# A decoder block with seven-product matmuls: sums of weight quarters made in DRAM for 54 units, and the first FFN block put in another order

## The chip, the core and the metric

The kernel runs on one core of a Trainium2 chip. The metric is the time of one execution on the device, in microseconds (us); lower is better. The core has five engines with an instruction queue each: TensorE (PE: matmuls; PEld: its weight loads), VectorE (DVE), ScalarE (ACT), GpSimd (POOL) and SyncE (SP). Data moves between DRAM and on-chip memory by DMA; here SP issues nearly all loads, POOL the stores of intermediate results and every DMA that adds to what its target holds.

## The reference

A decoder block for 512 rows of width 2048, in fp32. An input projection (2048 to 4096) feeds two token mixers (a gMLP spatial gate and an RG-LRU recurrence); their outputs go through an output projection. The channel mixer, which takes most of the time, is a GeGLU MLP with a causal convolution of width 3:

```python
h = _rmsnorm(x, norm2_g[l])
up = jnp.einsum('bsd,df->bsf', h, ffn_w_up[l])          # 2048 -> 12288
up = _causal_dwconv(up, ffn_conv_w[l], ffn_conv_b[l])
gate, val = jnp.split(up, 2, axis=-1)
x = x + jnp.einsum('bsf,fd->bsd', jax.nn.gelu(gate) * val, ffn_w_down[l])   # 6144 -> 2048
return _rmsnorm(x, final_g)
```

## The kernel before

**The mixers** (lines 240 to 563). Eight projections of 2048 x 512 and four output projections run as matmuls of 512 columns. In the first one (line 278) the rows of `xT`, the weights `w_in`, their splits and the squares for the norm all arrive piece by piece, and TensorE works on each as it comes (`load_rows`, lines 257 to 274; the loads alternate on SP's queue, lines 140 and 263).

**Precision.** Every fp32 operand is split into a rounded high part (`h`, a cast on ACT, line 115) and the rest (`l`, a subtraction on DVE, line 116), and each product is three matmuls.

**Seven products instead of eight.** In the FFN both operands are cut into 2 x 2 quarters, and a scheme of the Strassen-Winograd kind forms seven products of sums of quarters. A *unit* is one tile pair: 7 products x 2 halves x 3 matmuls of 256 columns (line 800), 42 matmuls. There are 280 units: 192 for the up projection (24 blocks of 8, gate and value in turn) and 88 for the down projection, in three chunks of 8, 8 and 6 row tiles by four column blocks. The last part of the down projection (lines 948 to 998) is plain matmuls.

**Operands.** A weight unit (class `Weights`) has a buffer `q` of eight slots: the four quarters of the weight in slots 4 to 7 and four sums in slots 0 to 3. `load` (line 579) issues the loads on SP, `sums` (line 587) makes the sums on DVE: lines 590 (two at once, 512 columns), 591 and 592 (256 each). `pair` (line 594) splits slots 0 to 6 into high and low parts of 1792 columns. Activations (class `Acts`) go the same way with differences (lines 615 to 617); for the first block they are filled by transposes on TensorE of the normed rows and a copy by ACT (`from_rows`, lines 706 and 708), for the down chunks loaded from `ad`, the DRAM buffer of gated activations. There are three buffers of `q` and three of the split weights, taken in turn.

**Sums made in DRAM.** For the last 96 units (184 to 279) the two sums of line 590 are not made on DVE: POOL copies two quarters into a DRAM tile `made` and adds the fourth quarter to both by an accumulating DMA (line 686), 256 KB each. One such DMA is issued per up unit, from unit 0 on, each adding one waiting for its copy. `load` then brings 256 KB from `made` and 384 KB from the weights.

**Order.** One list, `stream`, holds all operands in the order in which they are prepared. `prepare` (line 655) walks it: for each, load one ahead, sums one ahead, pair it, load two ahead. In the FFN each engine's queue is in the order in which this is written (line 773). The activations of a new chunk are spread over the units around the change, by `spread` (line 721); this and the units 0 to 7 are the three *changes of operand* and the *first up block*. Before the first block, units 0 to 2 are prepared during the output projection (line 760). Outside the part with a written order a scheduler places instructions; that holds for POOL at the start, too, where it puts the first `made` pieces ahead of the gate weights `graw` (line 336) of the recurrence.

Of the kernel before, what the change touches and what calls it, by code (L numbers as in the profile page):

```python
# [8 lines left out]
F32 = mybir.dt.float32  # L9
# [3 lines left out]
ALU = mybir.AluOpType  # L13

P = 128
S = 512
# [27 lines left out]
NG = 12  # L44
NP = 24

CHUNKS = [range(0, 8), range(8, 16), range(16, 22)]
TAIL = 22
# [15 lines left out]
EVAC = 150  # L64


@with_exitstack
def hybrid_block(ctx: ExitStack, tc: tile.TileContext, x, xT, w_in, w_out, w_up, w_dn, w_us, w_ds, w_dl, wab, wsT, vec, bs, vgb, fg, out):
# [399 lines left out]
    for i in range(2):  # L468
        for st in range(NS):
            t = vv[i][:, st]  # L470
# [97 lines left out]
    pools = {"t": pool("ts", "right")}  # L568

    def slots(name, n=8):  # L570
        return wq.tile([P, n, 256], F32, name=name, tag=name)

    class Weights:
# [5 lines left out]
        def load(self):  # L579
            self.q = q = slots("q")  # L580
            if self.made is None:
                nc.sync.dma_start(q[:, 4:8], self.src)
            else:
                nc.sync.dma_start(q[:, 2:4], self.made)
                nc.sync.dma_start(q[:, 4:7], self.src[:, 0:3])

        def sums(self):
            q = self.q
            if self.made is None:
                nc.vector.tensor_tensor(q[:, 2:4], q[:, 5:7], q[:, 7:8].broadcast_to([P, 2, 256]), ALU.add)  # L590
            nc.vector.tensor_tensor(q[:, 1], q[:, 2], q[:, 6], ALU.add)  # L591
            nc.vector.tensor_tensor(q[:, 0], q[:, 1], q[:, 4], ALU.add)  # L592

# [6 lines left out]
    class Acts:  # L600
# [45 lines left out]
    stream = []  # L646
    halves = []
    place, a_place = {}, {}
    done = [0, 0, 0]
# [18 lines left out]
    units = [(w_up[g + NG * v, m], m) for g, v in ups for m in range(8)]  # L668
    starts = []
    made = {}  # L670
# [3 lines left out]
    n_up = starts[0]  # L674


    sums_src = [w_us[m] for m in range(8)] + [w_ds[n, p] for c in CHUNKS for n in range(4) for p in c]
    for k, src in enumerate(sums_src):
        made[n_up - 8 + k] = tc.dram_tile([32, 2048], F32, name=f"made{k}")

    def make(u):

        k = u // 2
        if k < len(sums_src):
            how = {"accum_op": ALU.add, "max_dma_last_dim": 8192} if u % 2 else {"max_dma_last_dim": 8192}
            nc.gpsimd.dma_start(made[n_up - 8 + k], sums_src[k][u % 2], **how)  # L686

    def act_tiles(m, shape):
        a = pools["a2" if m == 7 else "a1"]
# [2 lines left out]
    def scale_rows(d):  # L692
        for st in range(NS):
            t = x2[d][:, st]
            if d < 2:
                nc.vector.tensor_scalar(t, t, rstd2[:, st:st + 1], None, ALU.mult)
            else:
                nc.scalar.mul(t, t, rstd2[:, st:st + 1])
# [38 lines left out]
    last_w = [Plain([w_dl[d].rearrange("p (a b) -> p a b", a=8)], half_tiles(i)) for i, d in enumerate(DORD)]  # L737
    for u, (src, _) in enumerate(units):
        place[u] = len(stream)
        stream.append(Weights(src, made[u].rearrange("(p b) (c d e) -> (p b c) d e", p=32, c=4, d=2) if u in made else None))  # L740
# [87 lines left out]
    def up_block(g, val, u0):  # L828
        q = {}
        for m in range(8):  # L830
            prepare(ready(u0 + m))
            for p in ORDER:
                product(q, p, act[m], stream[place[u0 + m]].hl, True, m == 0, m == 7)
                if p == 6:
                    rest_of_loads()
            make(u0 + m)
            if m == 7 and u0 == 0:
                pads[:] = [t_tile(f"pad{n}", [P, 2, S + 2]) for n in range(2)]
                for t in pads:
# [37 lines left out]
        for i, (n, j) in enumerate(((1, 0), (1, 1), (0, 0), (0, 1))):  # L877
            f = 48 * val + 4 * g + 2 * n + j
# [78 lines left out]
    for st in range(NS):  # L957
# [22 lines left out]
        v, y, u, r = (const.tile([P, 1], F32, name=f"r3{c}", tag=f"r3{c}", bufs=2) for c in "vyur")  # L980
# [80 lines left out]
```

## Time and profile before

| | us |
|---|---|
| median of 3 runs | 2106.33 (2104.26 to 2107.17) |
| the profiled execution | 2107.67, its span 2106.0 |
| TensorE matmul busy | 2048.9 (97%) |
| DVE busy | 1746.8 (83%) |
| ACT busy | 911.5 (43%) |
| mean granted TensorE clock | 0.987 |
| DMA, both directions | 338.08 MB, 161 GB/s on average |

Stages in the trace: mixers to about 562 us, first up block from 576 to 641, up blocks to about 1540, down blocks to 2051, the plain end to 2106. Busy time of TensorE comes from modelled ends of pipelined matmuls (284 ns each where they follow one another every 120 ns), so it says little; the number of matmuls in a window of known length says how far TensorE was held up. The granted clock tells when it ran at half speed. A row of the chain of waits has a start, a length and the engine, tile and line that the end of the program depended on then.

### The profile page before, as it was taken

To read this page: it belongs to the slowest core of one execution; us is meant where nothing else is said; L and a number is where in the kernel's file an instruction comes from. 1 tells how busy PE (TensorE), PEld (TensorE's weight loads), DVE (VectorE), ACT (ScalarE), POOL (GpSimd) and SP (SyncE) were. 2 spreads that over 40 slices of the span, in tenths; PEclk is the share of its full clock that TensorE was granted. 3 is DMA by queue.
4 is the path that set the end of the run, shared out by engine and by line. 5 is a ranking of instruction groups with operands and counts; after the bars stand their busy time and mean duration, and the time that the engine had idled before them with its cause. 6 is when DMAs were issued, how large, how long until landed. Compare 5 with 4: busy or idle time off the path is not lost.

```text
span 2106.0 us, 34882 instructions
## 1 busy us (share of the span) xinstructions
PE 2048.9 (97%) x14488; PEld 1928.0 (92%) x14488; DVE 1746.8 (83%) x2249; ACT 911.5 (43%) x899; POOL 185.9 (9%) x310
## 2 busy tenths in 40 slices
PE   9999999999889999999999999999988998999998
PEld 7888888888679999999999999999988998999996
DVE  7588972735379999999999999999989788778876
ACT  6445322413264444444444444444454344444443
POOL 1000000000010111111111112112110000000001
PEclk9999999999899999999999999999998999999999
DMA  8222322434133656556557557557565555645663
GB/s 276 89 84 95 102 100 100 160 104 166 70 103 118 175 152 185 163 161 188 155 166 195 161 156 200 152 156 198 164 190 175 206 177 193 233 163 202 231 235 120
DMA packets 91647, 338.08 MB, mean 161 GB/s; under 512 B 12768, under 2 KB 13408, under 8 KB 75616
## 3 DMA queue, kind: packets, MB, share of 16 engines
q1 hardware_dynamic: 71712, 236.60, 33.9%
q0 software_dynamic: 19200, 98.58, 17.0%
q8 instruction: 113, 1.85, 0.4%
q10 hardware_dynamic: 576, 0.66, 0.1%
q14 instruction: 46, 0.38, 0.1%
HBM read 304.34 MB, written 81.79 MB: 183 GB/s over the span
## 4 chain that ended last, share of the span: by engine, by line
PE 84%; DVE 10%; DMA 4%; issue 1%; ACT 1%; SPq 0%; DVEq 0%; ACTq 0%
PE qs L800 56%; PE ps L153 9%; PE ps L152 9%; PE ps L151 9%; DVE wl L116 3%; DVE al L116 2%; DMA q<-ad 1%; DMA q<-w_dn 1%; DMA q<-w_up 1%; DVE q L591 1%; DVE q L615 1%; PE qs L152 1%; PE qs L153 1%; PE qs L151 1%; DVE q L592 0%
## 5 line engine op out<-in xcount | busy, mean ns | idle before, releaser
L800 PE MATMUL qs<-al,wh 128*128 128x256 f32 x2688 | 763.8, 284 | 3.6 <-DVE al L116 3.5
L800 PE MATMUL qs<-ah,wh 128*128 128x256 f32 x2688 | 764.4, 284 | 2.7 <-DVE pad L817 1.8
L800 PE MATMUL qs<-ah,wl 128*128 128x256 f32 x2688 | 763.4, 284 | 2.8 <-DVE wl L116 2.8
L115 ACT CAST wh<-q 128x1792 fp32r<-128x1792 f32 (+1 forms) x282 | 476.7, 1691 | 651.1 <-PE qs L800 474.6
L116 DVE TENSOR_TENSOR wl<-q,wh 128x1792 fp32r<-128x1792 f32 (+1 forms) x282 | 567.9, 2014 | 55.4 <-ACT wh L115 55.1
L800 PEld LDWEIGHTS qs<-al,wh 128*128 128x128 f32 x2688 | 518.8, 193 | 4.5 <-DVE al L116 4.5
L800 PEld LDWEIGHTS qs<-ah,wh 128*128 128x128 f32 x2688 | 518.8, 193 | 3.2 <-DVE pad L817 2.0
L800 PEld LDWEIGHTS qs<-ah,wl 128*128 128x128 f32 x2688 | 518.7, 193 | 3.2 <-DVE wl L116 3.2
L800 PE MATMUL qs<-wh,ah 128*128 128x256 f32 x1232 | 353.7, 287 | 11.0 <-ACT cc L913 4.5
L800 PE MATMUL qs<-wl,ah 128*128 128x256 f32 x1232 | 353.7, 287 | 7.4 <-DVE wl L116 7.4
L800 PE MATMUL qs<-wh,al 128*128 128x256 f32 x1232 | 352.9, 286 | 3.9 <-DVE al L116 3.9
L800 PEld LDWEIGHTS qs<-wh,ah 128*128 128x128 f32 x1232 | 240.9, 196 | 12.2 <-ACT cc L913 4.9
L800 PEld LDWEIGHTS qs<-wl,ah 128*128 128x128 f32 x1232 | 240.9, 196 | 9.2 <-DVE wl L116 9.2
L800 PEld LDWEIGHTS qs<-wh,al 128*128 128x128 f32 x1232 | 240.8, 195 | 4.3 <-DVE al L116 4.3
L116 DVE TENSOR_TENSOR wl<-wraw,wh 128x1024 fp32r<-128x1024 f32 (+2 forms) x105 | 118.2, 1126 | 147.6 <-ACT wh L115 147.2
L115 ACT CAST wh<-wraw 128x1024 fp32r<-128x1024 f32 (+2 forms) x105 | 102.2, 975 | 272.2 <-PE ps L152 141.0
L151 PE MATMUL ps<-xgh,wh 128*128 128x512 f32 x384 | 152.5, 398 | 0.1
L152 PE MATMUL ps<-xgl,wh 128*128 128x512 f32 x384 | 152.2, 397 | 0.0
L153 PE MATMUL ps<-xgh,wl 128*128 128x512 f32 x384 | 150.5, 397 | 0.1
L591 DVE TENSOR_TENSOR q<-q 128x256 f32<-128x256 f32 x280 | 118.6, 424 | 29.7 <-DMA q<-w_dn 20.1
L686 POOL DMA_DIRECT2D made<-w_ds x176 | 115.3, 755 | 283.0 <-DMA made<-w_ds 273.8
L590 DVE TENSOR_TENSOR q<-q 128x512 f32<-128x512 f32 x184 | 126.1, 685 | 6.4 <-DMA q<-w_up 6.2
(244 smaller groups left out, 2418.5 us busy)
## 6 DMA issues: line engine op xcount, KB each, us to landing
q<-w_up SPq DMA_DIRECT2D x184, 512.0 KB, 3.6
made<-w_ds POOLq DMA_DIRECT2D x176, 256.0 KB, 4.4
q<-w_dn SPq DMA_DIRECT2D x88, 384.0 KB, 3.3
wraw<-w_in SPq DMA_DIRECT2D x28, 1024.0 KB, 4.8
q<-made SPq DMA_DIRECT2D x96, 256.0 KB, 2.6
wraw<-w_out SPq DMA_DIRECT2D x16, 1024.0 KB, 4.8
ad<-gate POOLq DMA_DIRECT2D x48, 256.0 KB, 2.4
q<-ad SPq DMA_DIRECT2D x24, 512.0 KB, 3.3
```

Of the source, the lines that this page charges most:

```text
L115: nc.scalar.copy(h, src)
L116: nc.vector.tensor_tensor(l, src, h.bitcast(F32), ALU.subtract)
L151: nc.tensor.matmul(ps, lhsT=ah, rhs=bh, start=start, stop=False)
L152: nc.tensor.matmul(ps, lhsT=ah, rhs=bl, start=False, stop=False)
L153: nc.tensor.matmul(ps, lhsT=al, rhs=bh, start=False, stop=stop)
L590: nc.vector.tensor_tensor(q[:, 2:4], q[:, 5:7], q[:, 7:8].broadcast_to([P, 2, 256]), ALU.add)
L591: nc.vector.tensor_tensor(q[:, 1], q[:, 2], q[:, 6], ALU.add)
L615: nc.vector.tensor_tensor(q[:, 2:4], q[:, 7:8].broadcast_to([P, 2, 256]), q[:, 5:7], ALU.subtract)
L686: nc.gpsimd.dma_start(made[n_up - 8 + k], sums_src[k][u % 2], **how)
L800: nc.tensor.matmul(q[p][:, t], lhsT=x_, rhs=y_, start=first and t == 0 and n == 0, stop=last and t == 1 and n == 2, skip_group_check=True)
```

## The change

1. For 54 units all four sums are made in DRAM: units 0 to 7, and around each chunk's start the eight units before it and the chunk's first column block. Their tile `made` has 512 KB, put together by four DMAs on POOL: a copy of 512 KB and additions of 512, 256 and 128 KB. Their `load` brings 512 KB from `made` and 384 KB of quarters, and `sums` does nothing. The other 50 units of the last 88 keep two sums, as before. Pieces of four units take turns, so that an addition does not directly follow the piece on which it waits.
2. The 32 pieces for units 0 to 7 are issued at the kernel's start; the other 284 two per up unit.
3. In the first block a second operand of activations is built and a third begun before the first product; the scalings of two further row groups come one operand later; 40 matmuls into an unused bank (`idle`) stand ahead of the first transposes.
4. `spread` is denser: the eight activations of a new chunk take 11 units instead of 13.

```diff
+def made_units():
+    n_up = 24 * 8
+    starts = [n_up + 4 * (c[0] - CHUNKS[0][0]) for c in CHUNKS]
+    whole = list(range(8))
+    for c, s in zip(CHUNKS, starts):
+        whole += range(s - 8, s + len(c))
+    end = starts[-1] + 4 * len(CHUNKS[-1])
+    return whole, [u for u in range(n_up, end) if u not in whole]
...
-                nc.sync.dma_start(q[:, 2:4], self.made)
+                nc.sync.dma_start(q[:, 4 - self.made.shape[1]:4], self.made)
                 nc.sync.dma_start(q[:, 4:7], self.src[:, 0:3])
...
                 nc.vector.tensor_tensor(q[:, 2:4], q[:, 5:7], q[:, 7:8].broadcast_to([P, 2, 256]), ALU.add)
+            elif self.made.shape[1] == 4:
+                return
             nc.vector.tensor_tensor(q[:, 1], q[:, 2], q[:, 6], ALU.add)
...
-            if self.fill is not None and self.m in (1, 3):
-                scale_rows(2 + self.m // 2)
+            if self.fill is not None and self.m in (2, 4):
+                scale_rows(1 + self.m // 2)
...
-    def make(u):
-
-        k = u // 2
-        if k < len(sums_src):
-            how = {"accum_op": ALU.add, "max_dma_last_dim": 8192} if u % 2 else {"max_dma_last_dim": 8192}
-            nc.gpsimd.dma_start(made[n_up - 8 + k], sums_src[k][u % 2], **how)
+    for k, u in enumerate(whole):
+        t = tc.dram_tile([P, 4, 256], F32, name=f"made{u}")
+        made[u], rows[u] = t, [
+            (t.rearrange("(a b) c d -> a (b c d)", b=2), w_m4[k, 0:512].rearrange("(a b) c -> a (b c)", b=8)),
+            (t.rearrange("(a b) c d -> a (b c d)", b=2), w_m4[k, 512:1024].rearrange("(a b) c -> a (b c)", b=8)),
+            (t[:, 0:2], w_m4[k, 1024:1280].rearrange("(p a) c -> p a c", p=P)),
+            (t[:, 0], w_m4[k, 1280:1408]),
+        ]
...
+    for i in range(8, len(order), 4):
+        group = order[i:i + 4]
+        to_make += [(r, *rows[u][r]) for r in range(4) for u in group if r < len(rows[u])]
+    start_make = [(r, *rows[u][r]) for r in range(4) for u in order[:8]]
+
+    def make(todo, n):
+
+        for _ in range(min(n, len(todo))):
+            r, dst, src = todo.pop(0)
+            how = {"accum_op": ALU.add} if r else {}
+            nc.gpsimd.dma_start(dst, src, max_dma_last_dim=8192, **how)
+
+    make(start_make, len(start_make))
...
-    spread = (0, 2, 3, 5, 7, 9, 10, 12)
+    spread = (0, 1, 3, 4, 6, 7, 9, 10)
...
+    idle = pools["tr"].tile([P, S], F32, name="tr", tag="tr")
+    for _ in range(40):
+        nc.tensor.matmul(idle[:, 0:256], lhsT=stream[0].hl[0][:, 0, 0:P], rhs=stream[0].hl[0][:, 1], start=True, stop=True)
     first = a_place[0]
     stream[first].load()
...
     rest_of_loads()
-    done[:] = [first + 2, first + 1, first + 1]
+    stream[first + 1].sums()
+    stream[first + 1].pair()
+    stream[first + 2].load()
+    done[:] = [first + 3, first + 2, first + 2]
...
-            make(u0 + m)
+            make(to_make, 2)
```

The host hands over copies of the weight quarters in the order in which the pieces read them (`w_m4`, `w_m2`); it adds nothing up.

How the change moves instructions is shown at three places. Lines in rows of the changed kernel are its own; a number behind a name tells buffers apart.

POOL's queue at the start, before (`made` is the DRAM tile of sums, `graw` the gate weights of the recurrence, `pad` the zeroed edge of a convolution buffer):

```order
L686 DMA made_3491<-w_us 32x2048
masks.py:199 ISA
masks.py:199 AFFINE_SELECT ident<-ident 128x128
L686 DMA made_3491<-w_us 32x2048
L686 DMA made_3492<-w_us 32x2048 x2
L686 DMA made_3493<-w_us 32x2048 x2
L686 DMA made_3494<-w_us 32x2048 x2
L336 DMA graw<-wab 128x256
L313 MEMSET pad 128x3 x4
L336 DMA graw<-wab 128x256 x4
```

And in the changed kernel:

```order
L717 DMA made0_3491<-w_m4 64x2048
masks.py:199 ISA
masks.py:199 AFFINE_SELECT ident_88<-ident_88 128x128
L717 DMA made1_3492<-w_m4 64x2048
...
L717 DMA made7_3498<-w_m4 64x2048
L717 DMA made0_3491<-w_m4 64x2048
...
L717 DMA made5_3496<-w_m4 64x2048
L347 DMA graw_590<-wab 128x256
...
L347 DMA graw_702<-wab 128x256
L717 DMA made6_3497<-w_m4 64x2048
```

Eight pieces of 256 KB stood ahead of the first gate weights; now eight copies and six additions of 512 KB do. Behind the second `graw` stand the remaining 18 pieces of units 0 to 7 and four copies for units 184 to 187, and only then the third `graw`.

DVE in the first block, before (`al`, `wl`: low parts of activations and weights; sums of weights are lines 590 to 592, of activations 615 to 617):

```order
L116 TENSOR_TENSOR al2_4302<-q_4269,ah2_4301 128x1792
L615 TENSOR_TENSOR q_4305<-q_4305 128x512
L616 TENSOR_TENSOR q_4305<-q_4305 128x256
L617 TENSOR_TENSOR q_4305<-q_4305 128x256
L116 TENSOR_TENSOR wl_4365<-q_4296,wh_4364 128x1792
L590 TENSOR_TENSOR q_4368<-q_4368 128x512
L591 TENSOR_TENSOR q_4368<-q_4368 128x256
L592 TENSOR_TENSOR q_4368<-q_4368 128x256
L116 TENSOR_TENSOR al3_4374<-q_4305,ah3_4373 128x1792
```

And in the changed kernel:

```order
L127 TENSOR_TENSOR al2_4372<-q_4301,ah2_4371 128x1792
L628 TENSOR_TENSOR q_4379<-q_4379 128x512
L629 TENSOR_TENSOR q_4379<-q_4379 128x256
L630 TENSOR_TENSOR q_4379<-q_4379 128x256
L127 TENSOR_TENSOR wl_4440<-q_4365,wh_4439 128x1792
L127 TENSOR_TENSOR al3_4447<-q_4379,ah3_4446 128x1792
```

The three sums of the weight unit are gone from between the split of a weight and the split of an activation.

TensorE at the start of the first block, before (`tr` is the bank of the transposes, `qs` that of a product):

```order
L706 MATMUL tr_4183<-ident_88,x2_2805 128x128 x4
L706 MATMUL tr_4189<-ident_88,x2_2805 128x128 x4
L706 MATMUL tr_4207<-ident_88,x2_2805 128x128 x4
L706 MATMUL tr_4213<-ident_88,x2_2805 128x128 x4
L800 MATMUL qs_4219<-ah0_4202,wh_3987 128x256
```

And in the changed kernel:

```order
L812 MATMUL tr_4216<-wh_4023 128x256 x40
L739 MATMUL tr_4258<-ident_88,x2_2805 128x128 x4
L739 MATMUL tr_4264<-ident_88,x2_2805 128x128 x4
L739 MATMUL tr_4282<-ident_88,x2_2805 128x128 x4
L739 MATMUL tr_4288<-ident_88,x2_2805 128x128 x4
L739 MATMUL tr_4302<-ident_88,x2_3053 128x128 x4
L840 MATMUL qs_4308<-ah0_4277,wh_4023 128x256
```

The 40 idle matmuls come first, and the first transposes of the third operand now stand ahead of the first product; before, three transposes stood between unit 0 and unit 1, and now one does.

More of the change, by code (lines that the diff above doesn't have):

```diff
@@ L64, with hybrid_block @@
 EVAC = 150
+def made_units():
[6 more added lines that the diff above has]
+    return whole, [u for u in range(n_up, end) if u not in whole]
 @with_exitstack
-def hybrid_block(ctx: ExitStack, tc: tile.TileContext, x, xT, w_in, w_out, w_up, w_dn, w_us, w_ds, w_dl, wab, wsT, vec, bs, vgb, fg, out):
+def hybrid_block(ctx: ExitStack, tc: tile.TileContext, x, xT, w_in, w_out, w_up, w_dn, w_m4, w_m2, w_dl, wab, wsT, vec, bs, vgb, fg, out):
     nc = tc.nc
@@ L739, in hybrid_block @@
         place[u] = len(stream)
-        stream.append(Weights(src, made[u].rearrange("(p b) (c d e) -> (p b c) d e", p=32, c=4, d=2) if u in made else None))
+        stream.append(Weights(src, made.get(u)))
         for a in after.get(u, ()):
@@ L1021, in quarters, with made @@
         return c(np.stack([b[:, :, :, 0, 1], b[:, :, :, 0, 0], b[:, :, :, 1, 1], b[:, :, :, 1, 0]], axis=3))
-    def pairs(w):
-        q = quarters(w)
-        return c(np.stack([q[:, :, :, 1:3], q[:, :, :, [3, 3]]], axis=2)).reshape(*q.shape[:2], 2, 32, 2048)
+    w_up, w_dn = quarters(i["ffn_w_up"][0]), quarters(i["ffn_w_down"][0][:TAIL * 2 * P])
+    units = [w_up[g + NG * v, m] for g in range(NG) for v in range(2) for m in range(8)]
+    units += [w_dn[n, p] for ch in CHUNKS for n in range(4) for p in ch]
+    whole, halved = made_units()
+    def made(us, lists):
+        return c(np.stack([np.concatenate([units[u][:, list(q)].reshape(-1, 256) for q in lists]) for u in us]))
     vec = np.concatenate(
@@ L1041 @@
         "w_out": c(i["w_out"][0].reshape(4, 4, P, 4, 512).transpose(3, 0, 2, 1, 4)).reshape(4, 4, P, 2048),
-        "w_up": quarters(i["ffn_w_up"][0]),
-        "w_dn": quarters(i["ffn_w_down"][0][:TAIL * 2 * P]),
-        "w_us": pairs(i["ffn_w_up"][0])[23],
-        "w_ds": pairs(i["ffn_w_down"][0][:TAIL * 2 * P]),
+        "w_up": w_up,
+        "w_dn": w_dn,
+        "w_m4": made(whole, [(0, 2, 1, 2), (3, 3, 3, 3), (1, 1), (2,)]),
+        "w_m2": made(halved, [(1, 2), (3, 3)]),
         "w_dl": c(i["ffn_w_down"][0][TAIL * 2 * P:].reshape(4, P, 4, 512).transpose(2, 1, 0, 3)).reshape(4, P, 2048),
```

11 lines of the change are left out of this document (8 added, 3 removed).

## The prediction

> **What bounds the kernel now.** I read the chain of waits first, then matmul counts per stage, then what DVE does where counts fall short.
>
> ```profile
> PE 84%; DVE 10%; DMA 4%; issue 1%; ACT 1%; SPq 0%; DVEq 0%; ACTq 0%
> ```
>
> TensorE is the chain for 84% of the span; only the rest can be won. Line 800 (the FFN products), counted in five windows (us; busy; matmuls; granted clock; DMA share; GB/s):
>
> ```profile
> 1200.00:1280.00 80.00, 80.00 (x669) 1.00 0.60 169
> 1550.00:1630.00 80.00, 67.22 (x494) 0.89 0.52 170
> 1740.00:1810.00 70.00, 60.94 (x481) 0.98 0.61 204
> 1920.00:1960.00 40.00, 36.82 (x290) 0.96 0.52 179
> 561.00:641.00 80.00, 49.09 (x342) 0.85 0.36 106
> ```
>
> Undisturbed, 669 matmuls fit into 80 us: 0.12 us each, so a unit (42 matmuls) takes 5.03 us. Against that rate the three changes of operand miss 175, 104 and 44 matmuls, which is 21.0, 12.5 and 5.3 us, 38.8 us together. The 80 us around the first up block miss 327, or 39 us, part of it the norm ahead of it. In the first row, as in the other up blocks, nothing is missing: DVE work saved there is worth nothing.
>
> Who is late at those places? DVE (third pair of numbers) is busy for 73 of 80 us at the first change:
>
> ```profile
> 1550.00:1630.00 80.00, 67.22 (x494) 65.58 (x492) 73.13 (x89) 40.15 (x32) 4.05 (x7) 0.89 0.52 170
> L116 DVE TENSOR_TENSOR wl<-q,wh 128x1792 fp32r<-128x1792 f32 (+1 forms) x282 | 567.9, 2014 | 55.4 <-ACT wh L115 55.1
> L590 DVE TENSOR_TENSOR q<-q 128x512 f32<-128x512 f32 x184 | 126.1, 685 | 6.4 <-DMA q<-w_up 6.2
> L591 DVE TENSOR_TENSOR q<-q 128x256 f32<-128x256 f32 x280 | 118.6, 424 | 29.7 <-DMA q<-w_dn 20.1
> L115 ACT CAST wh<-q 128x1792 fp32r<-128x1792 f32 (+1 forms) x282 | 476.7, 1691 | 651.1 <-PE qs L800 474.6
> L615 DVE TENSOR_TENSOR q<-q 128x512 f32<-128x512 f32 x5 | 3.4, 688 | 2.5 <-ACT q L708 2.5
> L864 DVE SCALAR_TENSOR_TENSOR gate<-pad,vc,gate 128x512 f32<-128x512 f32 x8 | 6.0, 750 | 0.1
> L820 DVE TENSOR_TENSOR w<-qs,v 128x512 f32<-128x512 f32 x2 | 1.4, 692 | 0.2
> ```
>
> A plain weight unit costs DVE 0.69 + 2 x 0.42 + 2.01 = 3.55 us, a half-made one 2.87 (line 590 falls away), a wholly made one 2.01. An operand of activations costs 0.69 + 0.85 + 2.01 = 3.55.
>
> **The changes of operand.** First change before, 14 units: 14 x 2.87 + 8 operands x 3.55 + two combines of 7 x 0.69 + some 15 us of taps (line 864, 16 times, and the products) = 93 us on DVE, where TensorE needs 70: 23 over, 21.0 lost. After, the eight operands stand in about 12 units: 24 + 28 + 10 + 13 = 75 us against 60: 15 over. Shorter stalls also cost less at a lowered clock (0.89 here), so I take 10 us lost: -11. Second: 13 x 2.87 + 28 + two evacuations of some 7.3 = 80 against 65 before, 65 against 55 after: 5 us less, -5. Third, with six operands: -1. Sum **-17**. Bounds: the saved sums alone, 0.85 x (14 + 13 + 10) = 31 us, cannot give back more than is lost, and denser operands take part: -27 at best. At worst the loads decide. A whole unit loads 512 + 384 KB, where it was 256 + 384:
>
> ```profile
> q<-w_up SPq DMA_DIRECT2D x184, 512.0 KB, 3.6
> q<-made SPq DMA_DIRECT2D x96, 256.0 KB, 2.6
> q<-w_dn SPq DMA_DIRECT2D x88, 384.0 KB, 3.3
> wraw<-w_in SPq DMA_DIRECT2D x28, 1024.0 KB, 4.8
> 1742.59 7.56 DMA q<-ad
> ```
>
> By the sizes beside it, 896 KB land in about 4.5 us alone. Three slots of `q` turn, so three items need one pass of load, cast and split: (4.5 + 1.7 + 2.0) for a weight, (3.6 + 1.5 + 1.7 + 2.0) for an operand, 2.8 us per item; 19 items in 11 units are 4.9 us per unit, just under 5.03. With both near the 7 us and more of the last row, met at the second change, it is 3.9, a unit takes 6.7, and only some 3 us are won: -3 is the other end.
>
> **The first up block.** The chain of waits there (start, length, who):
>
> ```profile
> 566.58 1.66 PE L706 MATMUL tr<-ident,x 128*128 128x128 f32 x4 [4.58 <-DVE x L696]
> 576.39 7.43 PE qs L800 x41
> 585.04 0.67 PE tr L706 x4
> 588.10 2.04 DVE al L116
> 590.17 4.00 PE qs L800 x17
> 619.41 3.62 DMA q<-w_up
> 626.62 3.51 DMA q<-w_up
> 641.47 3.67 PE qs L800 x21
> ```
>
> Eight units take 65.1 us (576.39 to 641.47) where they need 40.3 and their transposes. Step by step: (a) the 40 idle matmuls (40 x 0.12 = 4.8 us, in the 4.58 us in which TensorE now stands idle ahead of 566.58) keep the clock up, so the first transposes take 0.67 instead of 1.66; one more transpose group now stands ahead of the products: start 0.9 us earlier. (b) Operand 1 is now built on DVE during unit 0, so the stop between unit 0 (ends 583.8) and 590.17, 6.3 us, goes, with the 2 us that the next 17 matmuls lost at half clock (4.00 against 2.04): -8.3. (c) From 619.41 to 626.62 a unit took 7.2 us: load, sums, split of the operand in a ring. Without weight sums DVE needs 1.54 + 2 x 2.01 = 5.6; TensorE with two transpose groups 5.03 + 2 x 0.65 = 6.3 sets the pace. Five units: -4. (d) The two scalings of rows on ACT, now one operand later, stand ahead of two evacuations of transposes, and at the end of the block DVE still has units 8 to 10 to build with plain sums, so the combine waits: +2. Together **-11**. Bounds: -15 if (d) is free; -5 if the loads take over, since two units are one ring of load + 1.7 + 2.0 + 2.0, which passes 12.6 us at a load of 7, and the making of sums now runs beside it from about 590 with 512 KB pieces.
>
> The clock has a row to weigh. In the stop from 583.8 to 590.17 it fell to half (the 17 matmuls in 4.00 us) although three groups of transposes, 0.67 us each, ran in it; by that the sparse transposes after 567 do not hold it, and unit 0 still starts slow. The Trainium skill (TensorE: Matmul & The Clock Gate, Part 1) has the clock drop after an idle window of about 3.4 us. Taken by the letter, no window would be idle here and unit 0 would keep full clock, 7.43 - 4.92 = 2.5 us more, an estimate; I keep the row.
>
> **The start.** All 32 pieces for units 0 to 7 now go first on POOL's queue. Before, 8 pieces of 256 KB stood ahead of the first gate weights; now 14 of 512 KB. They share the transfer engines with the loads that feed the first projection:
>
> ```profile
> 1.72 4.42 DMA wraw<-w_in
> 8.00:33.00 25.00, 24.90 (x106) 19.59 (x105) 24.02 (x38) 22.79 (x41) 5.20 (x12) 1.00 1.04 355
> q1 hardware_dynamic: 643, 1.17, 104.0%
> q0 software_dynamic: 95, 0.52, 61.8%
> q1 hardware_dynamic: 256, 0.46, 40.8%
> 22.04 1.45 SPq L263 DMA_DIRECT2D xt<-xT  x2
> 73.40 0.40 ACT L115 CAST gah<-graw 128x256 fp32r<-128x256 f32 x1
> POOL made L686 <- DMA made<-w_us: 38.6, 8, 6.8
> ```
>
> The second row: TensorE, DVE, ACT and the engines of DMA (1.04) are all full from 8 to 33 us, so what comes late is not made up. The q1 rows are loads, q0 the sums: 14 to 17 us moved 1.17 MB with no sums, 18 to 21 us 0.46 MB beside 0.52 MB of sums. So 1 MB of sums takes 0.71 / 0.52 = 1.37 MB of loads away, 3.5 us at 0.39 MB/us. The extra 14 x 0.524 - 8 x 0.262 = 5.24 MB take 18 us. The loads lead: the last rows of `xT`, issued at 22.04 and about 8 us under way, are needed with step 11 of 16 (106 matmuls in 25 us, 12 per step, 2.8 us), near 40, less 3 for splitting: some 6 us of lead there, 4 at step 5. Later pieces wait behind POOL's gate weights, whose slots come free only as rows are used up. Bounds 0 (all inside the lead or the POOL waits) and +14; I take **+9**. Behind the waiting pieces on POOL stand the gate weights; the third is wanted by ACT at 73.40, later by the delay itself; the 13.6 MB ahead of it need some 62 to 80 us at the 0.17 MB/us of that row and the 0.22 of the next part: just hidden, and up to 4 us if not, which the upper bound holds.
>
> **The up phase.** Making runs beside plain loads, now two pieces per unit until unit 142, up to 512 KB each. All engines in a quiet stretch; the two queues in 28 us with sums (720 to 748); the plain loads' landing over all up blocks:
>
> ```profile
> 1200.00:1280.00 80.00, 80.00 (x669) 80.00 (x668) 76.76 (x98) 36.44 (x30) 12.61 (x20) 1.00 0.60 169
> q0 software_dynamic: 480, 2.62, 43.0%
> q1 hardware_dynamic: 862, 3.14, 34.2%
> DMA to landing us min/median/max: 3.3/3.6/5.9
> ```
>
> 0.43 x 28 / 2.62 = 4.6 us of all engines per MB of sums. Four whole units are 4 x 1.442 MB, 26.5 us, made in the time of 8 units, 40.2 us; their loads, 8 x 0.524 MB at 3.05 us, add 12.8: 39.3 of 40.2 us. Full, but only just. DVE is busy 76.76 of 80 us there, 4.83 per unit. Two units of its ring are one load, the sums and the split (3.55) and the other work (1.2): L + 4.7 us in 10.06, so a load may take 5.3 us before DVE falls behind. Bursts are covered: a unit is split (1.69 + 2.01 us) when TensorE frees one of three buffers, and used two units later, a lead of 6 us. I take **+2**; ends 0 and +29 (below).
>
> **Elsewhere**: units 0 to 2 lose their sums during the output projection, where TensorE is full: 0. The tail is unchanged: 0.
>
> **Sum**: +9 - 11 + 2 - 17 = -17 us. The profiled execution (2107.67 us, span 2106.0) is 1.3 above the median of 2106.33; differences go to the median: **2089**.
>
> **Rivals.** (1) *The start costs nothing*: the pieces run in gaps. For it, POOL waited 38.6 us for its own pieces (last row of the start), so they come in spurts; against it, the share of 1.04. -26: 2080. (2) *Making saturates the up phase*: 39.3 of 40.2 us leaves nothing. If plain loads land in 6 us instead of 3.6, two units of DVE's ring take 6 + 4.7 = 10.7 instead of 10.06, 0.3 us per unit, over 92 units with whole groups +29 instead of +2: 2116, slower. It decides above a median landing of 5.3 us. Against it, the row's maximum of 5.9 did no harm. The Trainium skill (DMA: Bandwidth & Descriptors, "Issuing engines are not separate DMA queues") says that all queues interleave on the same sixteen engines; by that rule, the trace agrees, no queue is spared. (3) *The loads take over* at the changes and in the first block: -3 and -5 instead of -17 and -11, with +9 and +2: +3, 2109, no change within the measurement.
>
> **Chances.** Forecast 0.58, rival 1 0.14, rival 2 0.16, rival 3 0.12. A difference of 0.2%, 4.2 us, is about what a measurement tells from none. Faster: nearly all of the forecast and rival 1, 0.70; same: rival 3's larger part and the forecast's edge, 0.11; slower: rival 2 and some of 3, 0.19. The likeliest case alone spans 2076 to 2101 (its bounds seldom fall together); with rivals 2 and 3 in part, 2073 to 2112.
>
> **What would show it.** Start: first projection's last matmul later by 5 to 14 us. First block: no stop after unit 0, about 6.3 us per unit. Up phase: still 669 matmuls per 80 us; landing of plain loads under 5.3. Changes: 85, 60 and 36 matmuls missing instead of 175, 104 and 44. Wrong if the up phase loses matmuls or the changes still miss 300 in all.

## The result: 4.3% slower, and the profile after

The changed kernel takes 2197.27 us (median of 4 runs, 2193.59 to 2198.81) where the kernel before took 2106.75 (2104.26 to 2108.14): a ratio of 1.0429, 95% interval 1.0410 to 1.0447. The forecast was 2089. In the profiled executions the span grew from 2106.0 to 2191.9 us, by 85.9. Stage by stage, in us:

| term | forecast | measured | from |
|---|---|---|---|
| start | +9 | +23.4 | start of the last matmul of the output projection, 561.6 and 585.0 |
| first up block | -11 | +1.7 | from there to the first combine, 79.1 and 80.8 |
| up phase, 720 to 1480 us | +2 | +83.1 | 693 matmuls missing at 0.12 us |
| changes of operand | -17 | -21.1 | 147 matmuls missing instead of 323 |
| sum | -17 | +87.1 | span: +85.9 |

TensorE's share of the chain of waits, 84% before, is now (changed kernel):

```profile
PE 44%; DVE 23%; DMA 17%; issue 14%; ACT 1%; POOL 1%; SPq 0%; DVEq 0%; ACTq 0%; POOLq 0%
```

**Start.** Windows of the changed kernel (us; busy time and count of PE, PEld, DVE, ACT, POOL; granted clock; DMA share; GB/s):

```profile
10.00:20.00 10.00, 5.35 (x13) 3.62 (x13) 2.07 (x4) 2.49 (x5) 3.51 (x5) 0.67 0.99 345
20.00:30.00 10.00, 6.95 (x19) 4.46 (x17) 2.05 (x3) 1.49 (x4) 0.00 (x0) 0.67 1.04 228
30.00:40.00 10.00, 4.46 (x11) 3.49 (x12) 2.65 (x4) 3.10 (x6) 0.00 (x0) 0.67 1.01 279
```

TensorE does 41 matmuls in these 30 us (one that runs across an edge is counted in both rows). Before, it did 132, and in the first of these windows 44:

```profile
10.00:20.00 10.00, 10.00 (x44) 8.05 (x43) 9.23 (x15) 8.99 (x16) 1.29 (x2) 1.00 1.02 337
```

The transfer engines are full in both. They are full of something else: queues (packets, MB, share) and loads (count, size, median us to landing) of the changed kernel from 10 to 20 us, and then the same of the kernel before.

```profile
q0 software_dynamic: 411, 2.69, 72.7%
q1 hardware_dynamic: 414, 0.76, 26.7%
xt<-xT SPq DMA_DIRECT2D x2, 256.0 KB, 25.8
wraw<-w_in SPq DMA_DIRECT2D x1, 256.0 KB, 21.8
```

```profile
q1 hardware_dynamic: 1355, 2.46, 68.3%
q0 software_dynamic: 158, 0.90, 33.9%
xt<-xT SPq DMA_DIRECT2D x6, 256.0 KB, 7.7
wraw<-w_in SPq DMA_DIRECT2D x4, 256.0 KB, 7.7
```

The loads (q1) fell from 2.46 MB to 0.76, and one took 22 to 26 us instead of 7.7.

**First up block.** The chain of the changed kernel: the stop after unit 0 is gone, but TensorE waits for two loads of `q`, 15.96 and 8.09 us long.

```profile
585.51 5.07 PE tr L812 x40
600.66 3.42 PE qs L840 x18
619.11 15.96 DMA q<-w_up
647.17 8.09 DMA q<-w_up
```

**Up phase.** The same 760 us of both kernels, first the kernel before (window; queues; landing of the plain loads of `q` there), then the changed one:

```profile
720.00:1480.00 760.00, 760.00 (x6336) 760.00 (x6335) 729.76 (x925) 344.24 (x285) 121.70 (x191) 1.00 0.61 172
q0 software_dynamic: 10320, 50.08, 27.7%
DMA to landing us min/median/max: 3.3/3.6/5.9
```

```profile
720.00:1480.00 760.00, 705.80 (x5643) 697.56 (x5642) 652.36 (x824) 305.86 (x250) 196.28 (x284) 0.97 0.77 210
q0 software_dynamic: 24384, 88.36, 50.2%
DMA to landing us min/median/max: 3.4/5.8/12.1
```

693 matmuls are missing. The mean DMA share of 0.77 looks harmless; two neighbouring stretches of 40 us do not. From 920 to 960 us the sums hold 75.7% of the engines and loads land in 8.1 us; from 960 to 1000 us, 36.6% and 4.3 us. Both stretches lose matmuls (281 and 276 of 336 are done). In the second one DVE is busy for 35.8 of the 40 us, and its sums wait 3.2 us for loads instead of 8.4: it seems to catch up on what the burst left undone, which these rows allow but don't prove. DVE's sum on line 601, which waited 6.2 us in all for plain loads before (as line 590), waits for 92 us (waits of the changed kernel: who, for what, us, times, longest):

```profile
q0 software_dynamic: 2188, 6.73, 75.7%
q<-w_up SPq DMA_DIRECT2D x6, 512.0 KB, 8.1
...
q0 software_dynamic: 1223, 3.69, 36.6%
q<-w_up SPq DMA_DIRECT2D x8, 512.0 KB, 4.3
```

```profile
DVE q L601 <- DMA q<-w_up: 92.0, 45, 6.4
```

**Changes of operand.** Of 1338, 335 and 335 matmuls that would fit into these windows of the changed kernel, 60, 43 and 44 are missing, 17.6 us where 38.8 were lost:

```profile
1600.00:1760.00 160.00, 155.45 (x1278) 154.63 (x1277) 141.80 (x156) 77.39 (x60) 6.45 (x12) 0.99 0.61 214
1840.00:1880.00 40.00, 36.24 (x292) 36.04 (x291) 35.34 (x37) 20.87 (x16) 0.54 (x1) 0.96 0.69 246
2000.00:2040.00 40.00, 36.44 (x291) 36.24 (x291) 33.35 (x35) 18.68 (x14) 1.07 (x2) 0.96 0.70 251
```

So the changes of operand paid as forecast. The time was lost elsewhere, at the start and in the up phase.

### The profile page after: what moved, and what is told of

Read it like the earlier page. It is cut to its first block, busy times and chain, and to the rows that moved or that the text cites. A ratio compares the mean times of both kernels' runs of the same rounds, so it can differ in the third digit from the quotient of the medians.

```text
span 2191.9 us, 35033 instructions
## 1 busy us (share of the span) xinstructions
PE 2077.0 (95%) x14528; PEld 1949.4 (89%) x14528; DVE 1703.5 (78%) x2133; ACT 911.8 (42%) x899; POOL 285.8 (13%) x434
## 4 chain that ended last, share of the span: by engine, by line
PE 44%; DVE 23%; DMA 17%; issue 14%; ACT 1%; POOL 1%; SPq 0%; DVEq 0%; ACTq 0%; POOLq 0%
PE qs L840 17%; DMA q<-w_up 12%; DVE wl L127 10%; PE ps L162 8%; PE ps L163 8%; PE ps L164 8%; DMA made<-w_m 3%; DVE q L601 3%; DVE q L604 2%; DVE cv L904 2%; DMA wraw<-w_in 1%; DMA q<-w_dn 1%; DVE gate L907 1%; DVE al L127 1%; DVE gate L904 1%
## 5 line engine op out<-in xcount | busy, mean ns | idle before, releaser
L840 PE MATMUL qs<-ah,wh 128*128 128x256 f32 x2688 | 774.5, 288 | 38.0 <-DVE pad L857 35.5
L840 PE MATMUL qs<-ah,wl 128*128 128x256 f32 x2688 | 772.0, 287 | 18.3 <-DVE wl L127 18.2
L840 PEld LDWEIGHTS qs<-ah,wh 128*128 128x128 f32 x2688 | 526.1, 196 | 42.9 <-DVE pad L857 39.0
L840 PEld LDWEIGHTS qs<-ah,wl 128*128 128x128 f32 x2688 | 525.8, 196 | 22.1 <-DVE wl L127 21.9
L840 PEld LDWEIGHTS qs<-al,wh 128*128 128x128 f32 x2688 | 526.0, 196 | 2.7 <-DVE al L127 2.7
L717 POOL DMA_DIRECT2D made<-w_m x316 | 225.3, 960 | 221.4 <-DMA made<-w_m 202.9
L601 DVE TENSOR_TENSOR q<-q 128x512 f32<-128x512 f32 x176 | 120.8, 686 | 92.2 <-DMA q<-w_up 92.0
L909 POOL DMA_DIRECT2D ad<-gate x48 | 27.5, 574 | 713.0 <-DVE gate L907 713.0
```

Of the source, the lines that this page charges most:

```text
L717: nc.gpsimd.dma_start(dst, src, max_dma_last_dim=8192, **how)
L840: nc.tensor.matmul(q[p][:, t], lhsT=x_, rhs=y_, start=first and t == 0 and n == 0, stop=last and t == 1 and n == 2, skip_group_check=True)
L909: nc.gpsimd.dma_start(ad[2 * g + n][:, at:at + 2], gate.rearrange("p (a b) -> p a b", a=2))
```

## The experiments

The numbers of all runs together. "First block" is the time from the start of the output projection's last matmul to the first combine; "missing" counts matmuls from 720 to 1480 us against the 6336 of the kernel before (100 are 12 us). The times of e7, e8, e10, e11 and e13 are medians of four to six runs; each other experiment is a single run. The kernel before, run beside the experiments, took 2106.86 to 2108.79 us (medians).

| run | us | last matmul of output projection | first block | missing |
|---|---|---|---|---|
| before | 2106.75 | 561.6 | 79.1 | 0 |
| changed | 2197.27 | 585.0 | 80.8 | 693 |
| e1_no_start | 2197.31 | 579.6 | 88.1 | 680 |
| e2_no_accum | 2140.19 | 580.5 | 74.1 | 304 |
| e3_paced | 2123.48 | 584.8 | 74.3 | 110 |
| e4_order_only | 2105.91 | 562.2 | 72.4 | 7 |
| e5_paced_no_start | 2102.75 | 562.2 | 75.0 | 166 |
| e6_pairs | 2165.40 | 585.1 | 75.5 | 461 |
| e7_fewer_paced | 2095.94 | 561.9 | 72.2 | 108 |
| e8_fewer_spread | 2090.19 | 562.0 | 72.5 | 93 |
| e9_loads_as_made | 2079.03 | 561.8 | 69.0 | 63 |
| e10_early | 2074.12 | 562.3 | 69.1 | 23 |
| e11_early_stretch | 2091.21 | 562.6 | 68.6 | 44 |
| e12_small_packets | 2173.97 | 583.0 | 80.1 | 528 |
| e13_early_small | 2076.37 | 562.8 | 69.2 | 57 |

The theory after the result: the sums' traffic takes the transfer engines from the loads. What of it does the harm was open: its place at the start, its volume, the additions as such, their bursts, or how deep they are queued.

**e1: no pieces for units 0 to 7.**

```diff
-    whole = list(range(8))
+    whole = []
...
-    start_make = [(r, *rows[u][r]) for r in range(4) for u in order[:8]]
-    make(start_make, len(start_make))
```

> Units 0 to 7 are not made in DRAM: no pieces at the kernel's start, their loads bring 512 KB, and DVE makes their sums as in the kernel before; all else is as in the changed kernel. Theory (the pieces at the start take the transfer engines from the loads of the first projection): the output projection ends near 562 us again instead of 585, time about 2197 - 23 = 2174; the first block stays near 65 us if the loads of q (619 and 647 us in the chain) are held up by the sums made for units 184 and on, which run beside it here too. Rival (the first block is slow because its loads grew from 512 to 896 KB): it falls to 55 to 58 us, time 2164 to 2167. Rival (the start is late for another reason than the pieces): no change, 2197.

The time did not move: 2197.31, the number of the last rival. But the edit did not free the start: the first 16 of the other pieces had nothing ahead of them on POOL any more and rose into the gap. Six of them stand between 2 and 10 us (issues of e1 in that window):

```profile
made<-w_m POOLq DMA_DIRECT2D x6, 512.0 KB, 8.8
```

All 16 went out before the gate weights: in the first 40 us POOL's queue moved 5.77 MB, where the changed kernel's moved 7.34. The output projection was still 18.0 us late, and the first block got longer. The experiment tells nothing against the theory; e5 repeats it with the pieces held back.

**e2: copies instead of additions.**

```diff
-            how = {"accum_op": ALU.add} if r else {}
+            how = {}
```

> The additions are replaced by plain copies of the same size into the same places, in the same order: what stands in made is then not the sum (the output is not the reference's), but as many pieces and bytes are handed over. Theory A (bytes saturate the transfer engines): the up phase still misses most of its 684 matmuls, time 2170 or more. Theory B (an addition holds a transfer engine about twice as long as a copy of the same size): the time that the making takes on the engines falls to about 0.6, the matmuls missing in the up phase fall below 250, the start is late by some 10 us instead of 23, time 2100 to 2135.

304 matmuls missing instead of 693: of the 83 us in the up phase some 47 come from adding, 36 remain for copies of the same bytes. Windows as above, of e2:

```profile
720.00:1480.00 760.00, 735.77 (x6032) 729.99 (x6031) 696.11 (x879) 328.03 (x269) 141.52 (x278) 0.99 0.64 214
DMA to landing us min/median/max: 3.4/3.9/9.4
```

Over the whole execution POOL's queue moved the same bytes in both (the queue's row on the page of the changed kernel, then of e2):

```profile
q0 software_dynamic: 38976, 152.33, 27.1%
```

```profile
q0 software_dynamic: 30336, 152.33, 20.4%
```

That is 0.271 x 2191.9 = 594 us of all engines and 0.204 x 2138.5 = 436. Additions were 54 x 896 + 50 x 256 KB of it, 62.7 MB, so they cost 158 / 62.7 = 2.5 us per MB more than the 2.9 of a copy: 5.4 as an estimate, 1.9 times as much. The start gains less than theory B gave: 18.9 of its 23.4 us stay with plain copies. Theories A and B hold a part each, and the time meets neither range.

**e3: the same pieces at TensorE's pace.** Each up unit lets POOL send as many pieces as keep the bytes at 1/184 of all per unit; a one-element copy on ACT is what POOL waits for.

```diff
+        tick = ticks[u % 8]
+        nc.scalar.copy(tick, ones)
+        nc.gpsimd.memset(tick, 1.0)
+        while to_make and sent[0] < each * (u + 1):
+            sent[0] += kb(*to_make[0][:2])
+            make(to_make, 1)
...
-            make(to_make, 2)
+            make_by_bytes(u0 + m)
```

> The same pieces, start included, but POOL may issue them only at TensorE's pace and by bytes: per up unit a one-element copy on ACT, a one-element memset on POOL behind it, then as many pieces as bring the bytes sent to 1/184 of all per unit. Theory C (what hurts is that POOL runs up to 16 units ahead and the sums come in bursts of 73 to 77% of the transfer engines): the up phase loses less than 20 us instead of 82, time 2115 to 2140. Theory A (the sums are too much even when spread evenly): it still loses 50 us or more, time above 2165.

74 us came back. Window and queue of e3:

```profile
720.00:1480.00 760.00, 752.79 (x6226) 751.44 (x6225) 716.47 (x907) 349.72 (x425) 195.79 (x415) 0.99 0.83 214
q0 software_dynamic: 24336, 84.23, 51.8%
DMA to landing us min/median/max: 3.4/4.7/8.9
```

The sums have the same share of the engines as in the changed kernel (51.8 and 50.2%) and almost the same bytes; 110 matmuls are missing instead of 693. So neither volume nor additions alone do it; that they come in bursts does most of it. One rival is left for a part: the changed kernel sends its last piece at 1407 us, e3 at 1560, so the sums also come 13% faster. From 720 to 1400 us, where both make sums, 85 and 75 MB of them move, the engines are busy for 0.81 and 0.83, and 675 and 103 matmuls are missing. No run holds bursts and rate fully apart. But the paced runs (e3, e5, e7 to e11 and e13), with 64 to 84 MB from 720 to 1480 us, miss 23 to 166, so a rate 13% higher can hardly account for most of the difference. What a burst is shows in POOL's order of time in the changed kernel (start, length, instruction, idle time before it and what ended it):

```profile
927.12 0.59 POOL L909 DMA_DIRECT2D ad<-gate  x1 [5.93 <-DVE gate L907]
927.70 5.43 POOL L717 DMA_DIRECT2D made<-w_m  x8
...
963.90 2.84 POOL L717 DMA_DIRECT2D made<-w_m  x5 [0.45 <-DMA made<-w_m]
995.44 0.56 POOL L909 DMA_DIRECT2D ad<-gate  x1 [28.70 <-DVE gate L907]
```

POOL's queue knows nothing of units. It sends eight pieces in 5.43 us once a store of activations has let it pass, goes on as pieces land, and then stands for 28.70 us before the next store.

**e4: the order of the first block alone**, on the kernel before.

> The kernel before with the new order of the first block alone (idle matmuls, second operand built ahead of the first product, scalings one operand later): two sums for 96 units, one piece per up unit, spread as before. My working: -11 us with the weight sums left to DVE it is less, as (a) and (b) alone give -9 and (c) needs the made sums: 2096 to 2100. Rival (the stops after unit 0 only move: the first block is bound by its loads and its operands' round trip whatever the order): within 3 us of before, 2103 to 2109.

The first block is 6.7 us shorter, as steps (a), (b) and (d) of the prediction have it (-7.2). The whole time, 2105.91 against 2107.41 beside it, shows little of that and lies in the rival's range: its three changes of operand miss 363 matmuls, 40 more than in the trace of before, nearly 5 us (178 of 1004 from 1520 to 1640 us, 123 of 669 from 1720, 62 of 335 from 1920). Whether that is the order's doing or chance is not settled.

**e5: e3 without pieces at the start.**

> As e3_paced (pieces issued at TensorE's pace and by bytes), and without the 32 pieces for units 0 to 7, whose sums DVE makes again: nothing at all stands on POOL's queue ahead of the gate weights. In e1_no_start other pieces had only moved up into their place. Theory (pieces at the start hold up the loads of the first projection): TensorE does some 160 matmuls in the first 40 us instead of 64, the output projection ends near 562 us, time 2123.5 - 23 = 2098 to 2103. Rival (the start is slow for another reason): 64 to 90 matmuls in the first 40 us, time 2115 or more.

The start is back (the first 40 us, e5, with 159 matmuls; e3 had 64), and with it 20.7 us:

```profile
0.00:40.00 40.00, 38.70 (x159) 31.01 (x160) 30.73 (x54) 29.21 (x53) 4.08 (x17) 1.00 0.80 267
```

**e6: pieces of two units in turn, not of four, not paced.**

```diff
-    for i in range(8, len(order), 4):
-        group = order[i:i + 4]
+    for i in range(8, len(order), 2):
+        group = order[i:i + 2]
```

> As the changed kernel, not paced, but after the start the pieces of two units take turns instead of those of four, so that an addition waits for the piece before last and about two are in flight. Pieces, bytes and start are the same. Theory C' (what makes the bursts is that four units' pieces are in flight at once): the up phase misses below 300 matmuls instead of 684, time 2130 to 2155. Rival (bytes and additions alone, however deep): over 500 missing, time 2175 to 2197; a further rival: POOL becomes late with its stores of gated activations, and time is lost at the first change of operand instead.

461 missing, between what the two theories gave: depth matters, since an addition that waits for the piece before last throttles POOL, but pace matters more (110).

**e7 and e8: fewer units, paced from unit 8 on; then the old spread.**

```diff
-        whole += range(s - 8, s + len(c))
+        whole += range(s - 5, s - 4 + (0, 1, 3, 4, 6, 7, 9, 10)[len(c) - 1])
```

> A version meant to be better than both: no pieces at the start, paced by bytes from unit 8 on, and all four sums only for the 30 units among which activations are prepared (5 before a chunk's start to 5 behind it, 2 behind for the third), two for the other 66; 78 MB of pieces instead of 92.5. By the runs so far: start 0, first block -6 (as with the new order alone), up phase +5 (15 lost when paced at 92.5 MB), changes -17: some 18 us under the kernel before, 2085 to 2093. If additions starve the loads even so: up phase +15, 2097 to 2102. If the 16 units left out matter: changes -8, about 2098.

> As e7_fewer_paced with the spread of activations of the kernel before (13 units instead of 11; the units with all four sums follow it, 36 instead of 30). Theory (the whole sums carry the gain at the changes, the spread is neutral): within 3 us of e7. Rival (the denser spread carries part of it): 5 to 10 us above e7. Rival (the denser spread is a loss, since it asks DVE for more per unit): 4 to 8 us below e7.

e7 is faster than the kernel before (ratio 0.9950, 0.9931 to 0.9970), by 11 us and not by 18; the up phase still misses 108, 13 us, near the 15 that the expectation gives for starved loads. e8 is at 0.9920 (0.9893 to 0.9946), 5.8 us under e7, though the two intervals overlap: the denser spread brings nothing that shows, and may cost. Its three changes miss 105 matmuls, e7's 158; e8 also has six more whole units, and the runs don't hold the two apart. The whole sums carry the gain at the changes: at the first one e8 misses 58 of 669 matmuls with the spread of before, where 175 were missing.

```profile
1560.00:1640.00 80.00, 75.82 (x611) 74.83 (x610) 73.25 (x80) 42.48 (x37) 3.73 (x10) 0.98 0.66 230
```

**e9: what the made sums are worth in the first block, without making them.**

```diff
-        stream.append(Weights(src, made.get(u)))
+        stream.append(Weights(src, w_m4[u, 0:512].rearrange("(p a) c -> p a c", p=P) if u < 8 else made.get(u)))
```

> As e8_fewer_spread, but units 0 to 7 load 512 + 384 KB as if their sums had been made, straight from the host's quarters, and nothing is made for them and DVE sums nothing (left out: the additions, so the output is not the reference's). It prices step (c) of the prediction alone, without its pieces. Theory (DVE sums are worth the 4 us that I gave them): from the end of the output projection to the first combine 68 to 69 us instead of 72.7. Rival (the larger loads take over, as the stops for q in the changed kernel suggest): 72 us or more. Whole time: 2087 +/- 5 less the gain.

The first block falls from 72.5 to 69.0: step (c), forecast at 4, is worth 3.5, and loads of 896 KB do no harm by themselves. The time, 2079.03, is 11 us under e8's median; the rest of that is more than the runs of e8 (2084.61 to 2094.37) let one explain.

**e10: the first 16 units' sums made while the mixers run**, between about 95 and 280 us, each tile first touched by a few bytes of the last gate weights so that the copy cannot start before them; the rest as in e8.

```diff
+    def make_early(n):
+        for r, dst, _ in early[:n]:
+            if r == 0:
+                late = dst[0:32, 0:1]
+                nc.gpsimd.dma_start(late, ga[7][1][0:32, 0, 0:1].bitcast(F32))
+        make(early, n)
```

> As e8_fewer_spread, and units 0 to 7 with all four sums again; their pieces and those of the next eight units (58 pieces, 24 MB) are made while the mixers run, none before the gate weights are split (a few bytes of these are first written into each tile, so that the copy has to wait for them, at about 95 us); the rest is paced over up units 8 to 184. Theory (sums cost nothing where loads leave the transfer engines three quarters free): mixers as before (output projection ends near 562 us), first block 3 to 4 us shorter than in e8, up phase 2 to 4 us better: 2081 to 2086. Rival (the pieces hold up w_in in the mixers as they did at the start): output projection later by 5 us or more, 2090 to 2105.

2074.12 us, ratio 0.9844 to the kernel before (0.9831 to 0.9856), better than forecast. The mixers from 100 to 280 us with the sums, and POOL's queue from 120 to 260 us, which shows 20 MB and not the 24 that I had written (e10); then the mixers without sums (the kernel before):

```profile
100.00:280.00 180.00, 180.00 (x772) 144.85 (x771) 156.66 (x152) 76.79 (x101) 52.28 (x78) 1.00 0.79 212
q0 software_dynamic: 6629, 20.40, 66.8%
```

```profile
100.00:280.00 180.00, 180.00 (x772) 144.88 (x771) 157.39 (x152) 76.68 (x101) 2.14 (x4) 1.00 0.29 99
```

Not one matmul is lost to a DMA share of 0.79. In the up phase 23 are missing (window; POOL's queue and the landing of the plain loads of `q` there):

```profile
720.00:1480.00 760.00, 758.79 (x6313) 757.74 (x6312) 727.48 (x922) 357.30 (x434) 175.21 (x391) 1.00 0.77 201
q0 software_dynamic: 19536, 73.02, 44.5%
DMA to landing us min/median/max: 3.3/4.4/8.8
```

The share of 0.77 there is that of the changed kernel, which lost 693; but the queue of the sums moved 73 MB in this window and not 88, since 20 MB had been made before, so e3 is the closer comparison for the bursts.

**e11: the rest stretched into the down phase** (paced over 204 units instead of 176).

> As e10_early with the rest paced over 204 units instead of 176, up to unit 212, some 28 units into the down phase. Theory (the loss in the up phase goes with the rate of the pieces): 1 to 3 us less than e10. Rival (the pieces meet the first change of operand and the loads of half-made units): 2 to 6 us more than e10.

The rival held, and the loss is larger than it said: 2091.21 (2084.48 to 2098.28), 17 us more than e10. The up phase gains nothing from the lower rate (44 missing), and at the first change the pieces meet the loads of half-made units. The same 80 us in e11 and in e10, with the landing of the weight quarters there, 5.9 and 4.0 us; 154 and 35 of 669 matmuls are missing:

```profile
1560.00:1640.00 80.00, 67.32 (x515) 65.58 (x515) 64.67 (x73) 37.18 (x41) 15.91 (x37) 0.94 0.80 263
q<-w_dn SPq DMA_DIRECT2D x14, 384.0 KB, 5.9
```

```profile
1560.00:1640.00 80.00, 76.98 (x634) 75.99 (x633) 72.91 (x81) 38.94 (x33) 4.58 (x10) 1.00 0.67 234
q<-w_dn SPq DMA_DIRECT2D x17, 384.0 KB, 4.0
```

**e12 and e13: rows of 2 KB in the pieces**, in the changed kernel and in e10.

```diff
-            nc.gpsimd.dma_start(dst, src, max_dma_last_dim=8192, **how)
+            nc.gpsimd.dma_start(dst, src, max_dma_last_dim=2048, **how)
```

> The changed kernel with its pieces cut into rows of 2 KB instead of 8 KB: the same pieces, bytes, order and start, four times the packets. In the changed kernel, from 10 to 30 us, the queue of the sums and that of the loads moved equally many packets (411 and 414, 272 and 267), but those of the sums are 6.5 KB on average and those of the loads 1.8. Theory D (the transfer engines take a packet from each queue in turn, so the loads' share is set by the size of the other queue's packets): TensorE does over 110 matmuls in the first 40 us instead of 63; the median landing of plain loads from 720 to 1480 us falls from 5.8 to below 4.8 us, and fewer than 400 matmuls are missing there instead of 693: 2130 to 2165. Rival (the share goes by the bytes that each queue has waiting): both as before, 2190 to 2200. Rival (the pieces get slower by their small packets, and POOL with writing them out): 2200 to 2260.

> e10_early with rows of 2 KB instead of 8 KB. Theory D: the up phase, where 23 matmuls were missing, loses nothing, 2068 to 2074. Rival (small packets cost the engines and POOL more than they give): 2080 to 2100.

The queues of e12 from 10 to 20 us:

```profile
q0 software_dynamic: 677, 2.47, 67.3%
q1 hardware_dynamic: 677, 1.23, 34.8%
```

Again both queues moved equally many packets, and the loads, 0.76 MB before the edit, now 1.23. The sums' packets are 3.6 KB on average there instead of 6.5. The packets are taken in turn; that much of theory D is shown. As a cure it is small, and none of the three numbers that theory D gave is reached: TensorE did 92 matmuls in the first 40 us instead of 63, 528 are missing in the up phase instead of 693, the median landing stays at 5.9 us (its maximum falls from 12.1 to 9.4), and the time falls by 23 us of the 90. Where pace has taken the bursts away, in e13, smaller packets bring nothing (2076.37 against 2074.12).

## Why the prediction was wrong

**The up phase** (+2, measured +83) is the step that failed. The sum "39.3 of 40.2 us" was made as if two pieces went with each unit, because they are written so, and the one sentence on bursts ("Bursts are covered", by a lead of 6 us) did not hold. The price of a piece in it was about right (4.6 us of all engines per MB there, 4.3 measured); the even spacing was not there. What TensorE feels is the landing of the load that is due next, and in a burst that is 8 us, beyond the 5.3 that the prediction itself gave as the limit. By the prediction's own ring, two units then take 8.1 + 4.7 = 12.8 us instead of 10.06, which uses up a lead of 6 us in four to five units (an estimate); the burst shown above goes on for 39 us. Averaging over a group of units hid it: about the same mean share costs 693 matmuls in the changed kernel and 110 in e3. Rival 2 had the mechanism and the point from which it decides (5.3; the median came to 5.8), but priced it at 29 us with one even landing of 6 us, where the maximum was 12.1. That additions cost 1.9 times as much as copies was inside the 4.6, and so not the error.

**The start** (+9, measured +23.4): 18 us of transfers less a lead of the loads. The lead was not there: loads that land after 22 us instead of 7.7 use up 6 us at once, and TensorE's granted clock fell to 0.67 in the gaps. The price per MB was low, too: the 5.24 MB of sums that came on top in the first 40 us cost 4.5 us each, the 3.67 MB of e1 4.9, against 3.5; with copies alone (e2) the 5.24 MB cost 18.9 us, 3.6 each, so by these traces what goes beyond the price comes from the additions. The prediction priced the loads' loss by bytes; they lose by packets: 411 against 414, but 6.5 KB against 1.8. The Trainium skill (DMA: Bandwidth & Descriptors, "Queues, rings and completion order") says that each transfer engine goes round the queues that have work and serves one whole packet of each; the counts above and those of e12 agree with it, if the profile counts packets as the page does, which no run here shows.

**The first block** (-11, measured +1.7): the steps were right and are worth 10.0 us when nothing is made beside them (e10, 79.1 to 69.1): (a), (b) and (d) 6.7 of 7.2 by e4, (c) 3.5 of 4 by e9. Only (a) had the wrong sign: the first product started 14.1 us after the output projection's last matmul before and 15.3 us in the changed kernel, since one more group of transposes stands ahead and the clock falls all the same (18 matmuls of unit 0 in 3.42 us, 0.19 each instead of 0.12). By the letter of the Trainium skill (TensorE: Matmul & The Clock Gate, Part 1), weighed in the prediction, unit 0 would have had full clock as I read it. It had not; TensorE stood for 3.35 us between the third and the fourth group of transposes (up to 597.65 us), and the fourth took 1.13 us where the second had taken 0.67. That gap is close to the idle window of about 3.4 us that the page means; whether it is one, no run here tells. What failed is the bound "-5 if the loads take over": it took a load of 7 us; the chain shows 15.96, with the pieces of later units beside it.

**The changes of operand** (-17, measured -21.1): right in mechanism, a little small; the denser spread, which I counted in, is not needed for it (e8, with the spread of before, misses 105 where the changed kernel misses 147).

**Elsewhere**: 0 as forecast.

## What to carry to other kernels

A background transfer is priced by the landing of the foreground load beside it, in its densest stretch and not on average; a queue runs as far ahead as its own waits let it, whatever unit its instructions are written in, so tie it to the engine that it must not disturb. Work for the transfer engines belongs where the next load has slack: here 20 MB in the mixers cost nothing, and 6 to 7 MB beside the first loads cost 18 to 23 us. When a piece of work is taken out at the head of a queue, look at what rises into its place.

## What the runs showed of the hardware

Two queues with work pending moved equally many packets, whatever their size (411 and 414, 677 and 677 in 10 us; e1, whose queue of sums ran low from 11 to 14 us, 249 and 504 from 10 to 20 us), so large packets on one queue take bytes from the other. An adding DMA from DRAM to DRAM held the transfer engines about 1.9 times as long as a copy of the same size (5.4 and 2.9 us of all engines per MB, an estimate from two whole executions). A DMA share of 0.79 cost no matmul in the mixers (e10); in the up phase, shares of 0.77 (e10) and 0.83 (e3) at an even pace cost 0.4% and 1.7% of the matmuls, and 0.77 in bursts cost 11%.
